# Products of constants in the first wait of the mixing stage and behind the sums of the output norms

## The chip, the cores and the metric

The kernel runs on one core of one Trainium2 chip. The time is that of one execution on the device, in microseconds; all rows below are of one profiled execution of the kernel before.

The core has a matrix engine (TensorE, PE in the profile; the loading of its weights is shown apart as PEld), a vector engine (DVE), a scalar engine (ACT), GpSimd (POOL), and SyncE (SP), which here only issues DMAs. The engines run side by side and wait for each other through semaphores. PE writes its results to PSUM, from which DVE and ACT read them. PE has a clock of two levels, 1.2 and 2.4 GHz; the profile shows which of them it was granted as 0.50 and 1.00.

## The reference

The kernel computes a hybrid decoder trunk of two layers on 256 tokens of width 1024, with 16 learned tokens ahead of them (T = 272). Each layer is a half-step SwiGLU feed-forward block, a token-mixing block, and a second half-step feed-forward block:

```
swiglu(x) = (silu(x @ w_gate) * (x @ w_up)) @ w_down
rms_norm(x, g) = x * rsqrt(mean(x * x) + EPS) * g
u = rms_norm(h, g_mix) @ w_in            # one projection, split into the inputs of four groups
A: rglru_mixer   B: gdn_mixer   C: ssd_mixer   D: s5_mixer
h = h + concat(yA, yB, yC, yD) @ w_out
```

The groups are a gated linear recurrence (A), a gated delta rule in chunks (B), a state-space scan in chunks (C) and a diagonal complex state-space model (D). Each ends in a norm of its own output: A over all its 512 channels, B over each of four heads of 128, C over two halves of 256. These are the output norms. All arithmetic is of float32 precision.

## The kernel before, in words

Activations lie with the channels on the 128 partitions and the tokens in the free dimension, so a product has 272 columns (256 in the second layer's end, where the learned tokens have been dropped). Weights stream in as pieces of 128x1024: SP loads `raw`, ACT rounds it to `hi` (L215), DVE takes the rest as `lo` (L217). A float32 product is made of three products of a reduced format that accumulate in one PSUM tile: `hi` with `xh` (L232), `hi` with `xl` (L233), `lo` with `xh` (L234); the helper is `mm3`. PSUM has eight banks: four for tiles `g` (weight products) and four for tiles `m` (all else, `s.mps()`).

The mixing stage is a list of steps, written out by hand. It begins with `first_tiles`, which puts the products of four output tiles on PE as far as the input is there, and then `norm_x` scales and splits the input: DVE multiplies (L315), ACT rounds (L316), DVE takes the rest (L317). The first four tiles are those of group D; DVE evicts them into `du` (L1158), which is stored and loaded again in another arrangement as `dU` (DMAs L1166 and L1168) and read by the products at L1179. The small tile of three scalar inputs per head is at L1290.

An output norm sums the squares over channels with products of one column (`token_sums`, L240: up to 128 tokens become the rows of the result, the constant `ones` is the moving operand). DVE adds epsilon (L251 or L253, tile `tok`), POOL takes the power of minus one half (L254, `toks`), PE brings the factor back to all partitions (`rstd_bc`, L262), and DVE multiplies (group A: L930; B: L777; C: L841). `ysplit` then rounds on ACT (L562, `s5a`) and takes the rest on DVE (L563, `s5b`), and the products of the output projection (`out_tiles`, L232 to L234) read these. In the list, the sums of a norm and its factor are separate steps (`an0` and `an1` for group A, `bo` with j = 0, 1, 2 for the heads of B, `cn` for C), with other work between them. Between the sums and the output products stand B's head products (L764 to L766), C's products (L826) and products of its decay (L517 to L525).

The order of the instructions on each engine comes from the list and from the framework's scheduler, which simulates the engines and moves instructions by priority. `issue_after(x)` pins what it encloses behind instruction x. The helper `fill` puts n products of the constant `onesr` (all ones) on PE, into a PSUM tile that nothing reads afterwards as such, behind `s.last_pe`. Before the change only `b_tail` set `s.last_pe`, and only `b_tail` with j = 1 called `fill`, with 5 products of 512 columns (L738).

PE runs its instructions in the order in which they are queued. The framework has a reader of a PSUM tile wait for the last PE instruction that wrote to the tile.

Of the kernel before, what the change touches and what calls it, by code (L numbers as in the profile page):

```python
# [16 lines left out]
P = 128  # L17
# [3 lines left out]
EPS = 1e-6  # L21
# [96 lines left out]
class Trunk:  # L118
# [110 lines left out]
    def mm3(s, ps, w, i, xh, xl, start, stop):  # L229
        nc = s.nc  # L230
        hi, lo = (t[:, i * P:(i + 1) * P] for t in w)
        nc.tensor.matmul(ps, lhsT=hi, rhs=xh, start=start, stop=False)  # L232
        nc.tensor.matmul(ps, lhsT=hi, rhs=xl, start=False, stop=False)  # L233
        nc.tensor.matmul(ps, lhsT=lo, rhs=xh, start=False, stop=stop)  # L234


    def token_sums(s, ps, acc, n, c=0, st=1):
        for b, o in enumerate(range(0, n, P)):
            w = min(P, n - o)
            s.nc.tensor.matmul(ps[0:w, c + b * st:c + b * st + 1], lhsT=acc[:, o:o + w], rhs=s.ones[:, 0:1], start=True, stop=True)  # L240


    def rstd_tok(s, ps, n, dim, eps, c=0, st=1):
# [18 lines left out]
            s.nc.tensor.matmul(pb[:, o:o + w], lhsT=rs[0:w, b:b + 1].to_broadcast([w, P]), rhs=s.ident[0:w, 0:w], start=True, stop=True)  # L262
        return pb[:, 0:n]

    def norm_tok(s, acc, n, dim, eps):
        ps = s.mps()
        s.token_sums(ps, acc, n)
        return s.rstd_tok(ps, n, dim, eps)

    def sumsq(s, acc, y, first, eng=None):  # L270
# [464 lines left out]
    def fill(s, ps, n):  # L735
        with s.tc.issue_after(s.last_pe):
            for _ in range(n):
                s.nc.tensor.matmul(ps, lhsT=s.onesr, rhs=s.onesr[:, 0:1].to_broadcast([P, 512]), start=True, stop=True)  # L738


    def b_tail(s, j):
# [16 lines left out]
    def b_out(s, h, l, j):  # L758
        nc = s.nc
        y = s.zb[:, h, :]  # L760
        if j == 0:
            ps = s.mps()
            n, o = s.N, T - s.N
            nc.tensor.matmul(ps[:, 0:n], lhsT=s.vs[:, 0, h, :], rhs=s.at[:, h, o:272], start=True, stop=False)  # L764
            nc.tensor.matmul(ps[:, 128 - o:n], lhsT=s.vs[:, 1, h, :], rhs=s.at[:, h, 272:416], start=False, stop=False)
            nc.tensor.matmul(ps[:, 256 - o:n], lhsT=s.vs[0:16, 2, h, :], rhs=s.at[0:16, h, 416:432], start=False, stop=True)  # L766
            t = s.buf('bt', [P, 4, T])[:, h, 0:n]
            nc.scalar.activation(out=t, in_=ps[:, 0:n], func=AF.Square)
            nc.vector.scalar_tensor_tensor(out=y, in0=ps[:, 0:n], scalar=s.gnh[:, l:l + 1], in1=y, op0=ALU.mult, op1=ALU.mult)
        elif j == 1:  # L770
            pn = s.mps()
            s.token_sums(pn, s.buf('bt', [P, 4, T])[:, h, :], s.N)
            s.bo[h] = s.rstd_tok(pn, s.N, 128, s.epq[:, :, h])
        else:
            pb = s.rstd_bc(s.bo[h], s.N)
            o = s.tmp()[:, 0:s.N]
            nc.vector.tensor_tensor(out=o, in0=y, in1=pb, op=ALU.mult)  # L777
            s.ysplit(o, 4 + h)
# [54 lines left out]

    def c_norm(s, g, l, j):
        if j == 0:
            s.cacc[g] = s.norm_tok(s.cacc[g], s.N, 256, 16 * EPS)
        else:
            pb = s.rstd_bc(s.cacc[g], s.N)
            for k in (2 * g, 2 * g + 1):
                o = s.tmp()[:, 0:s.N]  # L840
                s.nc.vector.scalar_tensor_tensor(out=o, in0=s.cy[:, k, :], scalar=s.col('snorm', l)[:, k:k + 1], in1=pb, op0=ALU.mult, op1=ALU.mult)  # L841
                s.ysplit(o, 8 + k)
# [78 lines left out]

    def a_norm(s, l, j):
        if j == 0:
            s.aacc = s.norm_tok(s.aacc, s.N, 512, 4 * EPS)
        else:
            s.ya = [s.rot([P, w], n, 1, F32R)[:, 0:4 * T] for n, w in (('s5a', 1840), ('s5b', 1792))]
            pb = s.rstd_bc(s.aacc, s.N)
            for i in range(4):
                o = s.tmp()[:, 0:s.N]
                s.nc.vector.scalar_tensor_tensor(out=o, in0=s.ag[:, i, :], scalar=s.col('lnorm', l)[:, i:i + 1], in1=pb, op0=ALU.mult, op1=ALU.mult)  # L930
                s.ysplit(o, i)
# [381 lines left out]
    def mixing(s, l, sl, done):  # L1313
        s.R, s.be, s.ce, s.bm, s.bo, s.cacc = ({} for _ in range(6))
        s5 = {}
        s.sl, s.N = sl, sl.stop - sl.start

        def small():
            s.sm16 = s.tokens(s.small_tile())

        def d_in(u):
            s5[u] = s.d_load(l, u)
            s.d_in(u, s5[u])

        def rin(i):
            s.R[i] = s.decay_in(i)

        def chain():
            with s.tc.issue_after(s.last_dve):
                s.b_chain()  # L1330

        do = dict(
            sm=small, tk=lambda: s.token_scalars(s.sm16, l), R=rin, S=lambda i: rin(2 + i),
            di=d_in, do=lambda u: s.d_out(u, s5[u]), da=lambda f: s.d_act(f, l), ds=s.d_split, dg=s.d_glu, dn=lambda j: s.d_norm(l, j),
            ks=lambda i: s.b_sums('k', i), qs=lambda i: s.b_sums('q', i), bn=lambda: s.b_norms(), bv=s.b_values, be=s.b_decay, bg=s.b_gram,
            bb=lambda: s.b_blocks(), bc=chain, bm=s.b_masks, bf=s.b_factor, bs=s.b_solve, bt=s.b_tail, bo=lambda h, j: s.b_out(h, l, j),
            xd=s.c_xdt, cg=s.c_gram, ce=s.c_decay, cp=lambda i: s.c_pair(i, l), cn=lambda g, j: s.c_norm(g, l, j),
            am=lambda i: s.a_gates(i, l), ac=lambda: s.a_coef(), an=lambda j: s.a_norm(l, j))
        do['as'] = s.a_scan
        full = slice(0, T)  # L1340
        pss = s.first_tiles(full)
        s.norm_x(s.col('nm', l), full)
        s.ahead(AHEAD)
        n, outs = 0, [0, 0]
        for name, a in STEPS:
            if name in IN:
                s.unit(name, a[0], pss[n] if n < NF else s.one_tile(sl if name in ('ag', 'bz', 'cz') else full), l)
                n += 1
            elif name in OUT:
                q = a[0]  # L1350
                s.out_tiles(q, OUT[name], outs[q] == 0, outs[q] == 3, sl, done)
                outs[q] += 1
            else:
                do[name](*a)
# [160 lines left out]
```

## Time and profile before

| | |
|---|---|
| median of 3 runs | 1443.67 us (1443.39 to 1445.18) |
| profiled execution | 1442.42 us |
| its span, from the first to the last instruction | 1440.5 us |
| mean granted clock of PE | 0.969 |
| PE busy | 1392.0 us, 97% of the span |
| DVE, ACT, POOL busy | 1036.4, 708.4, 205.4 us |
| L232, L233, L234 with `xh`, `xl` (2048 each) | 597.7, 595.3, 595.8 us |

The profile gives busy times by engine and line; a row of the timeline gives an instruction's start, its duration and, in brackets, how long its engine had been idle before it and for which instruction it had waited. PE instructions overlap: the time between the starts of two is what a product costs, and a duration holds its drain as well. A row with x4 is a run of four like instructions, its duration that of the run. The mixing stage of the first layer runs from about 235 to 500 us, that of the second from about 956 to 1215 us; the rest is feed-forward blocks.

### The profile page before, as it was taken

The page shows a single profiled execution, that of the slowest core. Times are in us where ns is not written, and L with a number is a line of the kernel's source. Part 1 is how long each engine was busy: PE and PEld are TensorE (multiplying, and loading weights), DVE is VectorE, ACT ScalarE, POOL GpSimd, SP SyncE. Part 2 cuts the span into 40 slices and gives each one's busy share as a digit, 9 for nine tenths or more (in the row PEclk, how much of TensorE's full clock was granted, in tenths as well). Part 3 has the DMA queues.
Part 4 walks back from the last instruction along what each step waited for, and adds up shares of the span by engine and source line. Part 5 has one row for each costly group of instructions (what it writes and reads, how often), then busy time and mean ns, then how long its engine had stood idle before and what let it go on. Part 6 is the DMA issues. An engine that isn't in the chain of part 4 may idle for free. (4 is left out here: it accounts for less than half of the span.)

```text
span 1440.5 us, 27604 instructions
## 1 busy us (share of the span) xinstructions
PE 1392.0 (97%) x10848; PEld 1353.8 (94%) x10848; DVE 1036.4 (72%) x1936; ACT 708.4 (49%) x1226; POOL 205.4 (14%) x235
## 2 busy tenths in 40 slices
PE   7999999998999999999999999999989899999997
PEld 7999998997998999999999999989989889999997
DVE  6998787978985468887656665669888746666653
ACT  6445444454675355554444444444555745544442
POOL 1000010322322320000100000103332223100011
PEclk9999999999997999999999999999999979999998
DMA  7568775654422256777555555556544213666662
GB/s 238 179 188 265 235 254 163 217 171 120 126 77 71 82 155 217 254 230 254 172 162 184 175 170 174 172 161 211 177 127 141 74 45 114 186 187 187 188 182 85
DMA packets 94025, 243.73 MB, mean 169 GB/s; under 512 B 29496, under 2 KB 39496, under 8 KB 93896
## 3 DMA queue, kind: packets, MB, share of 16 engines
q1 hardware_dynamic: 93896, 241.97, 54.2%
q8 instruction: 85, 1.39, 0.4%
q14 instruction: 44, 0.36, 0.1%
HBM read 222.16 MB, written 19.78 MB: 168 GB/s over the span
## 5 line engine op out<-in xcount | busy, mean ns | idle before, releaser
L215 ACT ACTIVATE hi<-raw 128x1024 fp32r<-128x1024 f32 (+1 forms) x382 | 403.3, 1056 | 532.2 <-PE g L233 302.0
L217 DVE TENSOR_TENSOR lo<-raw,hi 128x1024 fp32r<-128x1024 f32 (+1 forms) x382 | 470.2, 1231 | 215.6 <-ACT hi L215 213.9
L232 PE MATMUL g<-xh,hi 128*128 128x272 f32 (+1 forms) x2048 | 597.7, 293 | 12.2 <-ACT hi L215 8.7
L234 PE MATMUL g<-xh,lo 128*128 128x272 f32 (+1 forms) x2048 | 595.8, 292 | 0.8 <-DVE lo L217 0.8
L233 PE MATMUL g<-xl,hi 128*128 128x272 f32 (+1 forms) x2048 | 595.3, 291 | 0.3 <-DVE xl L317 0.3
L232 PEld LDWEIGHTS g<-xh,hi 128*128 128x128 f32 x2048 | 391.4, 191 | 14.7 <-ACT hi L215 8.6
L234 PEld LDWEIGHTS g<-xh,lo 128*128 128x128 f32 x2048 | 390.7, 191 | 2.6 <-DVE lo L217 1.1
L233 PEld LDWEIGHTS g<-xl,hi 128*128 128x128 f32 x2048 | 391.5, 191 | 1.5 <-DVE xl L317 0.6
L277 POOL TENSOR_TENSOR acc<-acc,r 128x272 f32<-128x272 f32 (+1 forms) x42 | 43.3, 1032 | 556.1 <-ACT r L276 555.4
L233 PE MATMUL g<-r,hi 128*128 128x272 f32 (+1 forms) x256 | 73.2, 286 | 0.0
L360 DVE TENSOR_TENSOR r<-r,g 128x272 f32<-128x272 f32 (+1 forms) x88 | 38.1, 432 | 37.5 <-PE g L234 36.0
L545 DVE SCALAR_TENSOR_TENSOR r<-g,small,r 128x269 f32<-128x269 f32 (+2 forms) x120 | 59.1, 493 | 2.0 <-ACT r L542 0.4
L234 PE MATMUL g<-ra,lo 128*128 128x272 f32 (+1 forms) x192 | 55.2, 287 | 0.0
L232 PE MATMUL g<-ra,hi 128*128 128x272 f32 (+1 forms) x192 | 55.1, 287 | 0.0
L233 PE MATMUL g<-rs,hi 128*128 128x272 f32 (+1 forms) x192 | 55.0, 286 | 0.0
L233 PE MATMUL g<-rz,hi 128*128 128x272 f32 (+1 forms) x192 | 55.0, 286 | 0.0
L234 PE MATMUL g<-rq,lo 128*128 128x272 f32 (+1 forms) x192 | 54.6, 287 | 0.0
L232 PE MATMUL g<-rq,hi 128*128 128x272 f32 (+1 forms) x192 | 53.5, 289 | 0.2
L358 DVE TENSOR_TENSOR r<-g,rstd 128x272 f32<-128x272 f32 (+1 forms) x88 | 38.3, 435 | 15.6 <-PE g L234 14.8
L233 PEld LDWEIGHTS g<-r,hi 128*128 128x128 f32 x256 | 48.1, 188 | 0.0
L232 PE MATMUL g<-dU,hi 128*128 128x272 f32 (+1 forms) x96 | 29.7, 309 | 9.8 <-DVE r L545 9.8
L359 ACT ACTIVATE r<-r 128x272 f32<-128x272 f32 (+1 forms) x88 | 36.5, 415 | 5.4 <-DVE r L358 4.2
(412 smaller groups left out, 2461.5 us busy)
## 6 DMA issues: line engine op xcount, KB each, us to landing
raw<-in_wgu_dram SPq DMA_DIRECT2D x176, 512.0 KB
raw<-in_wdn_dram SPq DMA_DIRECT2D x88, 512.0 KB
raw<-in_win_dram SPq DMA_DIRECT2D x80, 512.0 KB
raw<-in_wout_dram SPq DMA_DIRECT2D x32, 512.0 KB
s5a<-spill SPq DMA_DIRECT2D x8, 920.0 KB
s5b<-spill SPq DMA_DIRECT2D x8, 896.0 KB
spill<-s5a SPq DMA_DIRECT2D x8, 648.0 KB
spill<-rx SPq DMA_DIRECT2D x4, 640.0 KB
```

Source lines behind the costliest of these rows:

```text
L215: nc.scalar.activation(out=hi[:, 0:w], in_=raw[:, 0:w], func=AF.Copy)
L217: ins = nc.vector.tensor_tensor(out=lo[:, 0:w], in0=raw[:, 0:w], in1=hi[:, 0:w].bitcast(F32), op=ALU.subtract)
L232: nc.tensor.matmul(ps, lhsT=hi, rhs=xh, start=start, stop=False)
L233: nc.tensor.matmul(ps, lhsT=hi, rhs=xl, start=False, stop=False)
L234: nc.tensor.matmul(ps, lhsT=lo, rhs=xh, start=False, stop=stop)
L277: (eng or nc.gpsimd).tensor_tensor(out=acc, in0=acc, in1=t, op=ALU.add)
L358: nc.vector.tensor_tensor(out=t, in0=g[:, t0], in1=r, op=ALU.mult)
L359: nc.scalar.activation(out=si, in_=t, func=AF.Silu)
L360: nc.vector.tensor_tensor(out=a, in0=si, in1=u[:, t0], op=ALU.mult)
L545: nc.vector.scalar_tensor_tensor(out=dst[:, o:T], in0=ps[:, 0:T - o], scalar=taps[:, j:j + 1], in1=dst[:, o:T], op0=ALU.mult, op1=ALU.add)
```

## The change

`mm3` and `token_sums` now set `s.last_pe` too, and `fill` makes its products as wide as the PSUM piece it is given. Four products of 512 columns go into a fresh `m` tile between `first_tiles` and `norm_x`, in each layer. Three products of 384 columns go behind the sums of each output norm of groups A, B and C, into columns 128 to 511 of the sums' own PSUM tile: one group of three for A, four for B and two for C, so 7 groups in a layer. That makes 50 more products.

```diff
--- before.py
+++ after.py
@@ -231,13 +231,13 @@
         nc.tensor.matmul(ps, lhsT=hi, rhs=xl, start=False, stop=False)
-        nc.tensor.matmul(ps, lhsT=lo, rhs=xh, start=False, stop=stop)
+        s.last_pe = nc.tensor.matmul(ps, lhsT=lo, rhs=xh, start=False, stop=stop).ins
...
-            s.nc.tensor.matmul(ps[0:w, c + b * st:c + b * st + 1], lhsT=acc[:, o:o + w], rhs=s.ones[:, 0:1], start=True, stop=True)
+            s.last_pe = s.nc.tensor.matmul(ps[0:w, c + b * st:c + b * st + 1], lhsT=acc[:, o:o + w], rhs=s.ones[:, 0:1], start=True, stop=True).ins
@@ -262,9 +262,10 @@
-    def norm_tok(s, acc, n, dim, eps):
+    def norm_tok(s, acc, n, dim, eps, fill=0):
         ps = s.mps()
         s.token_sums(ps, acc, n)
+        s.fill(ps[:, 128:512], fill)
         return s.rstd_tok(ps, n, dim, eps)
@@ -735,7 +736,7 @@
     def fill(s, ps, n):
         with s.tc.issue_after(s.last_pe):
             for _ in range(n):
-                s.nc.tensor.matmul(ps, lhsT=s.onesr, rhs=s.onesr[:, 0:1].to_broadcast([P, 512]), start=True, stop=True)
+                s.nc.tensor.matmul(ps, lhsT=s.onesr, rhs=s.onesr[:, 0:1].to_broadcast([P, ps.shape[-1]]), start=True, stop=True)
@@ -770,6 +771,7 @@
             s.token_sums(pn, s.buf('bt', [P, 4, T])[:, h, :], s.N)
+            s.fill(pn[:, 128:512], 3)
...
-            s.cacc[g] = s.norm_tok(s.cacc[g], s.N, 256, 16 * EPS)
+            s.cacc[g] = s.norm_tok(s.cacc[g], s.N, 256, 16 * EPS, 3)
-            s.aacc = s.norm_tok(s.aacc, s.N, 512, 4 * EPS)
+            s.aacc = s.norm_tok(s.aacc, s.N, 512, 4 * EPS, 3)
@@ -1339,6 +1341,7 @@
         pss = s.first_tiles(full)
+        s.fill(s.mps(), 4)
         s.norm_x(s.col('nm', l), full)
```

Line numbers grow by one behind L265 and by two behind L773: the fill is at L738 before and at L739 after, the small tile at L1290 and L1292. Numbers in names count tiles and differ between the two kernels.

On PE, at the first wait of the first layer's mixing stage, the queue before reads as follows (`g_2960` is the last of the four first tiles, the other `g` tiles are the next ones):

```order
L234 MATMUL g_2960<-xh,lo_2954 128x272
L232 MATMUL g_2960<-xh,hi_2953 128x272
L233 MATMUL g_2960<-xl,hi_2953 128x272
L234 MATMUL g_2960<-xh,lo_2954 128x272
L232 MATMUL g_3134<-xh,hi_3106 128x272
L232 MATMUL g_3213<-xh,hi_3112 128x272
L1290 MATMUL g_3252<-xh,hi_3118 16x272
L233 MATMUL g_3134<-xl,hi_3106 128x272
```

Nothing stands between the last product of the first tiles and the first ones of the next. After the change, on the same engine at the same place:

```order
L234 MATMUL g_2960<-xh,lo_2954 128x272
L739 MATMUL m_3072<-onesr 128x512 x4
L232 MATMUL g_3139<-xh,hi_3111 128x272
L232 MATMUL g_3218<-xh,hi_3117 128x272
L1292 MATMUL g_3257<-xh,hi_3123 16x272
L233 MATMUL g_3139<-xl,hi_3111 128x272
```

The four products stand in the wait, and the rest is as it was. The second layer has them at the same place.

On PE, at the end of group B's solve and the sums of group A's norm (first layer), before (`m_5354` and `m_5447` are `b_tail`'s two tiles, `m_5516` that of the sums):

```order
L749 MATMUL m_5354<-rz_3283,rn_4060 16x128
L750 MATMUL m_5354<-rz_3283,rn_4060 16x128
L738 MATMUL m_5447<-onesr 128x512 x5
L764 MATMUL m_5498<-ra_4059,rs_4259 128x272
L765 MATMUL m_5498<-ra_4059,rs_4259 128x144
L826 MATMUL m_5504<-E_5042,rx_395 64x272 x2
L826 MATMUL m_5504<-E_5042,rx_395 64x144 x2
L826 MATMUL m_5504<-E_5042,rx_395 64x16 x2
L755 MATMUL m_5447<-rs_4259,a_72 16x128 x4
L240 MATMUL m_5516<-ones,cacc_5309 128x1 x2
L240 MATMUL m_5516<-ones,cacc_5309 16x1
L517 MATMUL m_5526<-r_5010,ugt 128x256
```

The five products stand behind the last of the pairs L749 and L750. After the change, from the first of these pairs on to the sums:

```order
L750 MATMUL m_5359<-rz_3288,rn_4065 16x128
L739 MATMUL m_5452<-onesr 128x512 x5
L751 MATMUL m_5359<-rz_3288,rn_4065 16x128
...
L756 MATMUL m_5452<-rs_4264,a_72 16x128 x4
L240 MATMUL m_5521<-ones,cacc_5314 128x1 x2
L240 MATMUL m_5521<-ones,cacc_5314 16x1
L739 MATMUL m_5521<-onesr 128x384 x3
L518 MATMUL m_5534<-r_5015,ugt 128x256
```

The old five products have moved seven products ahead, and three new ones stand behind the sums. Six more groups of this kind follow behind the other sums, and in the order after, the products of B's heads and C's (L765 to L767, L828) stand one by one between the first products of the output projection, where before they stood in one block behind 19 of them.

On PE, where the second layer's mixing stage reads `dU`, before (`g_11506` is a weight tile):

```order
L1290 MATMUL g_11472<-xl,hi_11338 16x272
L1290 MATMUL g_11472<-xh,lo_11339 16x272
L232 MATMUL g_11506<-xh,hi_11381 128x272
L233 MATMUL g_11506<-xl,hi_11381 128x272
L234 MATMUL g_11506<-xh,lo_11382 128x272
L232 MATMUL g_11506<-xh,hi_11381 128x272
L233 MATMUL g_11506<-xl,hi_11381 128x272
L234 MATMUL g_11506<-xh,lo_11382 128x272
L1179 MATMUL m_11399<-dU_7205,s5a_11395 128x68 x4
```

Six products of the tile stand ahead of L1179. After the change, at the same place:

```order
L233 MATMUL g_11537<-xl,hi_11412 128x272
L234 MATMUL g_11537<-xh,lo_11413 128x272
L232 MATMUL g_11537<-xh,hi_11412 128x272
L233 MATMUL g_11537<-xl,hi_11412 128x272
L234 MATMUL g_11537<-xh,lo_11413 128x272
L232 MATMUL g_11537<-xh,hi_11412 128x272
L233 MATMUL g_11537<-xl,hi_11412 128x272
L1181 MATMUL m_11430<-dU_7231,s5a_11426 128x68 x4
```

Thirteen products of that tile stand ahead of it there, of which the last seven are shown; in the first layer the order at this place is the same before and after.

## Rows read from the trace of the kernel before

**Rows 1.** Windows: stretch, length, busy time by engine, granted clock, DMA share, GB/s.

```profile
238.00:239.00 1.00, 0.76 (x3) 0.29 (x3) 1.00 (x4) 0.12 (x1) 0.00 (x0) 0.51 0.07 4
449.65:470.05 20.40, 20.07 (x74) 17.10 (x74) 5.06 (x17) 10.69 (x32) 6.97 (x9) 0.50 0.00 1
474.00:480.30 6.30, 6.30 (x55) 5.50 (x53) 4.58 (x12) 2.20 (x5) 5.39 (x6) 1.00 0.43 122
500.00:945.00 445.00, 445.00 (x3566) 441.85 (x3565) 301.05 (x439) 209.75 (x306) 22.30 (x29) 1.00 0.62 193
1166.45:1186.90 20.45, 19.04 (x69) 16.34 (x69) 4.75 (x15) 11.03 (x33) 5.71 (x5) 0.50 0.00 0
```

**Rows 2.** Timeline of PE: start, duration, engine, line, tiles, forms, idle before.

```profile
237.40 0.36 PE L232 MATMUL g<-xh,hi 128*128 128x272 f32 x1 [1.58 <-DVE du L1158]
...
238.95 0.59 PE L233 MATMUL g<-xl,hi 128*128 128x272 f32 x1
...
241.39 0.32 PE L234 MATMUL g<-xh,lo 128*128 128x272 f32 x1
...
249.46 0.78 PE L1179 MATMUL m<-dU,s5a 128*128 128x68 f32 x6
...
956.76 0.36 PE L232 MATMUL g<-xh,hi 128*128 128x272 f32 x1 [1.54 <-DVE du L1158]
...
969.89 1.97 PE L1179 MATMUL m<-dU,s5a 128*128 128x68 f32 x16 [0.39 <-DMA dU<-ud]
```

**Rows 3.** Timeline of PE at the first layer's output norms.

```profile
443.97 1.36 PE L738 MATMUL m<-onesr 128*128 128x512 f32 x5
...
448.01 0.74 PE L240 MATMUL m<-ones,cacc 128*128 128x1 f32 x6
...
449.43 0.44 PE L519 MATMUL m<-r,ugt 128*128 128x288 f32 x1
...
452.16 1.27 PE L764 MATMUL m<-ra,rs 128*128 128x272 f32 x2
...
454.38 1.27 PE L764 MATMUL m<-ra,rs 128*128 128x272 f32 x2
...
456.60 1.76 PE L262 MATMUL m<-cst,toks 128*128 128x128 f32 x6
...
459.41 1.27 PE L232 MATMUL g<-s5a,hi 128*128 128x272 f32 x4 [0.33 <-ACT s5a L562]
...
463.21 2.23 PE L240 MATMUL m<-ones,rz 128*128 128x1 f32 x12
465.37 0.59 PE L233 MATMUL g<-s5b,hi 128*128 128x272 f32 x1
...
469.84 0.77 PE L764 MATMUL m<-ra,rs 128*128 128x272 f32 x2
...
471.10 1.14 PE L826 MATMUL m<-E,rx 128*64 128x272 f32 x12
...
475.42 1.30 PE L240 MATMUL m<-ones,rz 128*128 128x1 f32 x12
...
477.72 1.03 PE L262 MATMUL m<-cst,toks 128*128 128x128 f32 x6
...
480.65 0.29 PE L519 MATMUL m<-r,ugt 128*128 128x288 f32 x1
...
482.27 0.77 PE L232 MATMUL g<-rq,hi 128*128 128x272 f32 x4
```

**Rows 4.** Chain that ended last, 955 to 975: start, duration, what.

```profile
964.89 4.87 DMA dU<-ud
```

**Rows 5.** Timeline of DVE at the first layer's output norms.

```profile
448.79 0.21 DVE L251 TENSOR_SCALAR tok<-m 128x2 f32<-128x2 f32 x2
...
458.39 1.72 DVE L930 SCALAR_TENSOR_TENSOR r<-dp,small,m 128x272 f32<-128x272 f32 x4 [7.92 <-PE m L262]
```

**Rows 6.** Timeline of PE at the second layer's output norms.

```profile
1176.74 0.58 PE L519 MATMUL m<-r,ugt 128*128 128x288 f32 x1 [1.42 <-DVE E L816]
```

## The prediction

> **What bounds the kernel now.** I read the windows first. In the stretch from 500 to 945, feed-forward blocks, PE is busy 445.00 of 445.00 us at a granted clock of 1.00, and 3566 products pass in it, 0.125 us each [rows 1]. There PE is the bound, so a product that is added to the path costs its full time, and what PE gains or loses in the mixing stage ahead of it comes out at the end. The windows then show where PE runs at the lower of its two clock levels (0.50, 1.2 GHz): about 1 us after the first wait of the mixing stage, where 238 to 239 has 0.51, and two long stretches at the output norms, 449.65 to 470.05 and 1166.45 to 1186.90, in which PE is busy 20.07 and 19.04 us, nearly always, and yet at 0.50 throughout [rows 1]. So the change meets three kinds of places: a wait in which PE does nothing, norm stages where it is busy at the lower level, and the same kind of work where it had the higher one.
>
> The timeline of PE says what went before each fall. In the first wait it had stood idle for 1.58 us (1.54 in the second layer) for DVE's eviction of `du` [rows 2]. At the norms it had not been idle. It ran six sums of one column from 448.01 on (0.74 us) and then B's decay from 449.43, and from 449.65 the clock is at 0.50 [rows 1, 3]. Yet from 474.00 to 480.30, with twelve such sums at 475.42 and six products L262 at 477.72, it is 1.00 all the time [rows 1, 3]; there weight products had filled PE behind C's products of 471.10. So such sums don't lower the clock wherever they stand: what lies around them decides, and products of constants are more of it.
>
> **The change part by part.** *First waits.* Four products of 512 columns cost 0.94 us (0.125 us for 272 columns gives 0.176 for 384 and 0.235 for 512). They fit into the idle 1.58 and 1.54 us, so they delay nothing: the products behind them wait for DVE, not for PE. If the clock stays, the 11 products from 238.95 to 241.39 take 1.38 instead of 2.44 us, 1.06 less [rows 2]. I take it that it stays: the pause shrinks to some 0.6 us. What is late next is `dU`. In the first layer L1179 starts at 249.46 without a wait of its own; in the second it waits 0.39 us for its reload, whose leg takes 4.87 us [rows 2, 4]. PE's clock doesn't bring the reload forward, since `du` hangs on DVE. In the first layer most of the gain becomes a wait there: I take -0.2 (bounds 0 and -1.06). In the second the order puts thirteen products instead of six ahead of L1179, 7 x 0.125 = 0.88 us, so PE comes there no sooner than now and keeps its gain: -1.0 (bounds 0 and -1.06). Sum -1.2.
>
> *A group of three at the norms* is 3 x 0.176 = 0.53 us at the higher level, 1.06 at the lower. In the first layer one group stands at 448.7, ahead of the fall, two behind the twelve sums at 463.21, four more behind 475; nothing covers them, since PE is busy there and stays the bound up to the end of the layer.
>
> *What the clock would give back*, if it stayed at 1.00 from 449.65 on, comes from like work at either level [rows 3]. B's decay products take 2.73 us from 449.43 to 452.16 and 1.62 from 480.65 to 482.27: 1.11 less, of which I take 0.9, since a first piece ran before the fall. The two blocks of B's head products take 2.22 each (452.16 to 454.38) against 1.26 (469.84 to 471.10): 1.92. Six products L262 take 1.76 against 1.03: 0.73. Four products L232 and B's decay again take 3.80 (459.41 to 463.21) against 4 x 0.125 + 1.62 = 2.12: 1.68. Twelve sums take 2.23 against 1.30: 0.93. Nineteen weight products take 4.47 (465.37 to 469.84) against 19 x 0.125 = 2.38: 2.09. Together 8.25 us. The second layer's stretch has the same length and pattern with 256 columns; I take the same sum.
>
> *Case by case, per layer.* Held throughout: 7 groups x 0.53 = 3.7 against 8.25, net -4.5. Held at first and lost in the wait behind L262: saved are 0.9 + 1.92 + 0.73 = 3.55; paid are 0.53 + 2 x 1.06 + 4 x 0.53 = 4.77; net +1.2. Lost as before: nothing saved, and 4.8 paid, net +4.8.
>
> *The wait behind L262* has no product of constants. The first L930 starts 1.8 us after L262 began, and PE's next product, L232, stands 0.33 us idle for ACT's rounding L562 [rows 3, 5]. At the higher level L262 and the two products behind it are over sooner, while DVE and ACT are not faster: from 458.39 to 459.41 their two steps take 1.02 us, of which PE would stand idle about 0.6 to 1.0. That lies between the idle 1.54 to 1.58 that lost the clock and the 0.39 at L1179 [rows 2]. In the second layer the products behind L262 stand idle 1.42 us for `E` [rows 6]. I count this as the point that decides, near to evens in each layer.
>
> *The norm's own chain.* DVE's `tok` (448.79, 0.1 us behind the sums) will wait for the last of the three products, as they go into the same tile: 0.53 us. Its factor L262 starts at 456.60, behind the two blocks of B [rows 3, 5]: DVE's 0.21 and POOL's power behind it leave some us in hand, and a faster PE, which comes to L262 about 2.3 us sooner, still leaves most of it. DVE then stands idle 7.92 us for L262 [rows 5], so nothing queued behind `tok` is pressed. I take 0 (at most 0.53 for the group). For B's sums the factor follows behind the weight products, at 477.72, 12 us later: 0.
>
> The row shows DVE reading the sums right behind PE. The Trainium skill ("PSUM — Partial Sum Buffer", section "PSUM bank collisions raise a hardware error") wants engines kept apart by bank and quadrant, not by address, which speaks against putting the products into columns 128 to 511 of the sums' tile: another address doesn't free DVE. By it, up to 7 x 0.53 = 3.7 us per layer could be added to the norm chains; by the rows it is hidden, for the first chain by the two blocks. No run here yet shows which.
>
> *Moved products.* `b_tail`'s five products move seven small products ahead; what `b_tail` does next doesn't come later by it: 0. B's head products and C's come earlier between the weight products of the output projection, also in PE's busy time: 0, with a bound of 1 us either way, as have the second layer's small changes of order on DVE, ACT and SP.
>
> **The sum.** One layer holds the clock and the other loses it behind L262: -1.2 - 4.5 + 1.2 = -4.5 us. The profiled execution took 1442.42 us (span 1440.5), so 1437.9; that execution lies 1.25 below the median of the runs, 1443.67, which gives 1439.2.
>
> **The rivals**, against the median:
> - *Both layers hold*: -1.2 - 9.0 = -10.2, 1433.5. For it: 474 to 480.3 has the same work and no product of constants, and held. Against it: the pauses behind L262 are unfilled.
> - *Both lose it behind L262*: -1.2 + 2.4 = +1.2, 1444.9. For it: the 1.42 us idle in the second layer, and the first four products there.
> - *One holds, one falls where it did*: -1.2 - 4.5 + 4.8 = -0.9, 1442.8. Three products are little against a stretch of several us of thin ones.
> - *The products only queue on a bound PE* (slower): the clock falls at the sums in both layers, or in one, with the other losing it later. Each layer then pays 4.8 (or 1.2 in that other): +8.4, 1452.1, or +4.8, 1448.5. For it: PE was busy at 0.50 for 20 us, so busy time alone doesn't keep the clock. It decides as soon as a norm stage is at 0.50 with its second and third group inside.
> - *The first waits don't keep the clock*: 1.2 worse in each case above; the pause that is left and the three partly idle products behind it speak for it. It shifts a case and makes none.
>
> **How the numbers follow.** Chances: forecast 0.36, both hold 0.25, both lose behind L262 0.12, one holds and one as before 0.10, the slower rival 0.17. The time is the forecast's, 1439.2; its own range, by the unknown moves and the first waits, is 1436 to 1443. The range for 8 in 10 reaches down through most of both-hold, 1431.5, and up into the slower rival, between its two sums, 1450. About 0.2%, 2.9 us, is what a measurement can tell here from no change: faster means below 1440.8, slower above 1446.6. Faster gets both-hold and some six tenths of the forecast, 0.45; the same gets the rest of the forecast and the two cases near zero, 0.29; slower gets the slower rival and the upper tail of those two, 0.26.
>
> **What would show it.** The clock in the windows 238 to 241 and 958 to 961 should be 1.00, and L1179 in the first layer should wait some 0.8 us for `dU`. At the norms the clock tells the case: 1.00 through both stretches, or a fall behind L262, or a fall at the sums. Products L240 and weight products next to each other should take their times at the level shown, and the three products 0.53 or 1.06. DVE's `tok` should begin some 0.5 us behind the sums and L262 wait for nothing. The forecast is wrong if the clock falls at the sums again, if the first waits still lose it, or if L262 comes to wait for `toks`.

## The result, and the profile after

The change makes the kernel slower: 1454.21 us median of 18 runs (1443.48 to 1459.21) against 1443.82 us of 18 runs before (1437.78 to 1450.27), ratio 1.0054, 95% interval 1.0037 to 1.0070. The ratio is not the quotient of the medians, which is 1.0072; executions of either kernel scatter by several us. Forecast were 1439.2 us and a range up to 1450. The profiled execution took 1457.68 us, with a span of 1456.0.

Windows of the changed kernel, columns as in [rows 1]:

```profile
238.00:241.00 3.00, 2.62 (x19) 2.11 (x19) 3.00 (x7) 0.00 (x0) 0.00 (x0) 1.00 0.60 172
250.90:257.70 6.80, 6.80 (x33) 6.80 (x32) 2.09 (x5) 0.35 (x2) 1.69 (x2) 0.50 0.34 134
455.70:476.20 20.50, 20.18 (x69) 16.55 (x67) 5.14 (x17) 10.97 (x33) 7.08 (x9) 0.50 0.00 1
1015.50:1025.70 10.20, 9.04 (x43) 9.04 (x43) 7.12 (x19) 4.86 (x14) 3.53 (x5) 0.50 0.71 234
1193.00:1199.80 6.80, 6.80 (x29) 6.62 (x29) 0.41 (x3) 1.72 (x7) 3.32 (x3) 0.50 0.00 0
```

Against [rows 1]: the first wait now runs at 1.00, and the 6.8 us from 250.9 on at 0.50, where the kernel before had 1.00. The first layer's norm stage has its 20.5 us at 0.50 as before. The second layer's has 6.8 instead of 20.45. The second layer's scan of group D has 10.2 us at 0.50, where the kernel before had 6.8:

```profile
1002.60:1009.40 6.80, 6.80 (x34) 6.80 (x33) 4.89 (x16) 4.85 (x14) 1.84 (x3) 0.50 0.85 278
```

PE's timeline at the first wait and at the reading of `dU`, columns as in [rows 2]:

```profile
235.54 1.03 PE L739 MATMUL m<-onesr 128*128 128x512 f32 x4
237.28 0.36 PE L232 MATMUL g<-xh,hi 128*128 128x272 f32 x1 [0.71 <-DVE du L1160]
...
250.26 3.09 PE L1181 MATMUL m<-dU,s5a 128*128 128x68 f32 x16 [1.88 <-DMA dU<-ud]
253.11 0.57 PE L234 MATMUL g<-xh,lo 128*128 128x272 f32 x1
```

The four products stand in the wait, as forecast, and the wait behind them shrinks from 1.58 to 0.71 us. PE is at the reading of `dU` by 248.38 and waits there 1.88 us, longer than the 1.06 us that the clock was to give, and behind that wait the clock falls: the sixteen products take 3.09 us and the next starts 2.85 us after the first.

PE's timeline at the first layer's output norms, then DVE's row that answers to the first of [rows 5], then the second layer's wait that answers to [rows 6]:

```profile
454.14 0.76 PE L739 MATMUL m<-onesr 128*128 128x384 f32 x3
454.74 0.39 PE L518 MATMUL m<-r,ugt 128*128 128x256 f32 x2
...
462.49 1.76 PE L262 MATMUL m<-cst,toks 128*128 128x128 f32 x6
...
470.33 1.32 PE L739 MATMUL m<-onesr 128*128 128x384 f32 x3
471.45 0.99 PE L240 MATMUL m<-ones,rz 128*128 128x1 f32 x6
...
483.27 0.76 PE L739 MATMUL m<-onesr 128*128 128x384 f32 x3
483.87 0.63 PE L240 MATMUL m<-ones,rz 128*128 128x1 f32 x6
```

```profile
454.94 0.21 DVE L251 TENSOR_SCALAR tok<-m 128x2 f32<-128x2 f32 x2 [0.68 <-PE m L739]
```

```profile
1190.26 0.37 PE L520 MATMUL m<-r,ugt 128*128 128x288 f32 x1 [1.60 <-DVE E L818]
```

A group of three costs PE 0.60 us at the higher level (454.14 to 454.74, 483.27 to 483.87) and 1.12 at the lower (470.33 to 471.45); forecast were 0.53 and 1.06. DVE waits 0.68 us for the group (forecast 0.53), and L262 stands without a wait, so that delay is hidden. The idle time that the forecast took as the point that decides is there (1.60 us in the second layer), and 2.7 us behind it the clock falls.

### The profile page after: what moved, and what is told of

Read it like the earlier page. It is cut to its first block, busy times and chain, and to the rows that moved or that the text cites. A ratio compares the mean times of both kernels' runs of the same rounds, so it can differ in the third digit from the quotient of the medians.

```text
span 1456.0 us, 27707 instructions
## 1 busy us (share of the span) xinstructions
PE 1402.8 (96%) x10898; PEld 1363.6 (94%) x10898; DVE 1037.0 (71%) x1936; ACT 708.0 (49%) x1226; POOL 204.6 (14%) x235
## 5 line engine op out<-in xcount | busy, mean ns | idle before, releaser
L361 DVE TENSOR_TENSOR r<-r,g 128x272 f32<-128x272 f32 (+1 forms) x88 | 38.0, 431 | 37.3 <-PE g L234 35.8
L359 DVE TENSOR_TENSOR r<-g,rstd 128x272 f32<-128x272 f32 (+1 forms) x88 | 38.1, 433 | 15.5 <-PE g L234 14.8
L552 ACT ACTIVATE r<-r 128x272 f32<-128x272 f32 x40 | 17.2, 429 | 47.4 <-DVE r L546 30.9
```

Of the source, the lines that this page charges most:

```text
L359: nc.vector.tensor_tensor(out=t, in0=g[:, t0], in1=r, op=ALU.mult)
L361: nc.vector.tensor_tensor(out=a, in0=si, in1=u[:, t0], op=ALU.mult)
L552: nc.scalar.activation(out=t, in_=x, func=AF.Tanh, scale=0.5)
```

## The experiments

Every kernel was run 6 to 18 times in turns with the kernel before. Beside time and ratio the table has two figures that each run gives: its time at 0.50, which is 2 x (1 - mean granted clock) x span, and the time without the clock's loss, which is the time less half of that (an estimate: it takes PE as the bound wherever the clock is low). Both are means over the runs. The kernel before was run anew beside each later batch: its medians there are 1443.98 to 1445.69, and 1398.7 to 1400.0 without the loss. A difference by the means is taken against the runs of before that stood beside the same kernel.

| kernel | median us | ratio, 95% interval | at 0.50 | without the loss |
|---|---|---|---|---|
| before (29 runs beside E1 to E4) | 1444.18 | 1 | 88.8 | 1399.8 |
| the change | 1454.21 | 1.0054 (1.0037 to 1.0070) | 82.3 | 1412.5 |
| E1 first waits only | 1445.88 | 1.0013 (0.9990 to 1.0037) | 90.8 | 1400.9 |
| E2 groups only | 1446.97 | 1.0027 (0.9998 to 1.0055) | 77.4 | 1409.2 |
| E3 moved five only | 1448.00 | 1.0023 (1.0000 to 1.0046) | 96.2 | 1399.8 |
| E4 the change again | 1455.96 | 1.0091 (1.0055 to 1.0128) | 86.3 | 1413.4 |
| E5 the change, five unmoved | 1446.11 | 1.0015 (0.9996 to 1.0035) | 73.3 | 1410.4 |
| E6 group A's sums only | 1442.31 | 0.9977 (0.9957 to 0.9998) | 79.7 | 1401.6 |
| E7 as E6, and four behind L262 | 1438.55 | 0.9953 (0.9932 to 0.9975) | 66.1 | 1404.7 |
| E8 groups of six only | 1456.24 | 1.0077 (1.0061 to 1.0094) | 74.6 | 1418.2 |
| E9 the change, no first waits | 1451.00 | 1.0051 (1.0028 to 1.0073) | 77.0 | 1411.9 |
| E10 E2, five moved in layer 2 | 1447.46 | 1.0030 (1.0001 to 1.0059) | 79.1 | 1408.4 |
| E11 five behind the sums | 1451.96 | 1.0059 (1.0035 to 1.0083) | 99.6 | 1401.6 |
| E12 as E7, with six | 1434.66 | 0.9946 (0.9919 to 0.9974) | 63.1 | 1404.2 |
| E13 the change, first wait in layer 1 only | 1452.25 | 1.0043 (1.0016 to 1.0071) | 78.1 | 1412.2 |
| E14 the same, in layer 2 only | 1453.75 | 1.0049 (1.0022 to 1.0075) | 79.8 | 1412.7 |
| E15 before again | 1444.74 | 0.9986 (0.9964 to 1.0008) | 87.7 | 1400.3 |
| E16 E12 again | 1436.34 | 0.9938 (0.9913 to 0.9962) | 64.3 | 1403.4 |
| E17 E2, five moved in layer 1 | 1449.72 | 1.0028 (1.0004 to 1.0052) | 77.7 | 1411.0 |
| E18 E5 again | 1450.36 | 1.0030 (1.0005 to 1.0054) | 80.6 | 1409.6 |

### E1 to E4: the parts alone

In E1, E2 and E5 the sums and the weight products set another attribute (`last_mm`), behind which the new products go, so `b_tail` keeps its place:

```diff
-        s.last_pe = nc.tensor.matmul(ps, lhsT=lo, rhs=xh, start=False, stop=stop).ins
+        s.last_mm = nc.tensor.matmul(ps, lhsT=lo, rhs=xh, start=False, stop=stop).ins
...
+        s.fill(s.mps(), 4, s.last_mm)      # E1, E5
+        s.fill(ps[:, 128:512], fill, s.last_mm)      # E2, E5
```

> Only the four products in each first wait; everything else as before the change. Theory 1 (early arrival at dU): the clock stays at 1.00 from 238 to 241, PE comes to L1179 about 1 us sooner, waits there 1 to 2 us for dU in the first layer, and the clock falls behind that wait; the time is 2 to 5 us longer than before. Theory 2 (the norms' products carry the whole loss): no fall at dU that costs more than it saves, time 0 to 2 us shorter. Theory 3 (the moved five products and the new order carry it): same as theory 2.

> Only the groups of three behind the sums; the five products of b_tail stay where they were before, and the first waits have none. Theory 1: the clock falls at the sums or behind L262 as it did before, 3 to 5 us more per layer where it falls at the sums and about -1 to +1 where it falls later; 4 to 8 us longer in all. Theory 2: 8 to 10 us longer. Theory 3: within 3 us of before.

E3 is the change without any new product; E4 the change itself.

> No new products; only the place of b_tail's five products and the order that the scheduler makes of it. Theories 1 and 2: within 2 us of before. Theory 3: 5 to 10 us longer, with the loss at the output norms and behind.

> The changed kernel once more, for a second profile of it. Theory 1: PE again waits over 1 us for dU in the first layer and the clock falls there; norms cost 3 to 5 us in a layer where the clock falls at the sums. If the places of the falls are chance, the wait at L1181 is there but the fall is not, and the layers differ from the first profile by several us each way; the time is 6 to 12 us above before in any case.

No part alone is clear of no change; E3's interval ends at it. E1 gains nothing: its time at 0.50 is about that of before. E2 has what the forecast was made for: the time at 0.50 falls by 11.4 us, which is worth 5.7, and 9.4 are paid for it. E3 pays nothing and has 7.4 us more at 0.50. Theories 2 and 3 fall as single causes: no part carries the loss, and the three means, 2.0, 3.6 and 3.6 us over before, come to about what the change costs, 9.2. E1's profile doesn't test theory 1: both first waits lost the clock in spite of the products (3.4 us each, from 239.3 and from 966.4), and PE didn't wait for `dU`. E4 has the wait for `dU` again, 1.99 us, with the fall behind it.

### E5, E18: the change without the moving

> The change, but with b_tail's five products where they stood before. Theory 1 (three separate costs that add: the first waits 2.0 us, the groups at the norms 3.6, the moved products 3.6): 5 to 6 us longer than before, and 3 to 5 us shorter than the changed kernel. Rival (the moved products cost nothing by themselves, the changed kernel's loss is that of the new products): as slow as the changed kernel, 9 to 10 us longer than before.

> The change with b_tail's five products where they stood before, a second sample and profile. Theory: the second layer's stretch from the small tile to the first b_tail product takes 200 to 203 us, PE waits for dz as in the kernel before; 2 to 4 us longer than before. Rival (the first sample was lucky): 5 us longer than before or more, that stretch over 204 us.

E5 and E18 are 2.7 and 4.4 us over before by their means (1447.0 and 1450.0 against 1444.3 and 1445.5), less than the 5 to 6 that E5's theory added up: new products alone cost some 3.6 us, and the moving in their company 4 to 7 more, up to the mean of the change (1453.7). E18's stretch in the second layer took 206.3 us, against the expectation, though PE's wait for `dz` is short; it waited 2.7 us for `dU` there, and the clock fell behind that wait too.

### E9, E10, E17: what the moving does

E9 is the change without the products in the first waits. E10 and E17 have the groups, and the move in one layer:

```diff
+        s.mv = l == 1      # E10; 0 in E17
+        if s.mv:
+            s.last_pe = s.last_mm
```

> The changed kernel without the products in the first waits: the groups of three and the moved five, in the changed kernel's order on every engine. Theory 1 (the first waits' products give little, 0 to 2 us either way; moving the five with the groups present costs the rest): 7 to 10 us longer than before, as the changed kernel within 2 us. Rival (the early arrival at dU makes the changed kernel slow): 3 to 5 us longer than before, like the groups alone.

> The groups of three, with b_tail's five products moved ahead in the second layer alone; the order on DVE, ACT, POOL and SP is that of the groups alone but for two rows. Theory 1a (the moving itself costs, by its place in each layer): 1.5 to 4 us longer than the groups alone, 5 to 8 longer than before. Theory 1b (what costs is the new order of the second layer's B and weight products, which comes with the moving in the first layer): within 1.5 us of the groups alone, 2.5 to 5 longer than before.

> The groups of three, with b_tail's five products moved ahead in the first layer alone. That move brings the changed kernel's new order of the second layer on all engines with it, the move in the second layer does not. Theory (the new order of the second layer is what costs, not the moving): the stretch from the second layer's small tile to its first b_tail product takes 204 to 206 us as in the five profiles with the new order, not 200 to 203 as in those without; PE waits over 3 us for dz there; 5 to 8 us longer than before, 2 to 4 longer than with the move in the second layer alone. Rival (the place of the five in the first layer costs at the norms): that stretch as before, the first layer's norm stage 3 us longer.

Moved in the second layer the five cost nothing over E2 (3.9 us over before against 3.6, by the means). Moved in the first layer, they make the scheduler order the second layer anew on PE, DVE and ACT, as it is in the change. The waits of PE from 960 to 1050, for `dz` of POOL (us in total, times, longest), in the change, in E17 and in E18, which has the old order there:

```profile
PE m L1217 <- POOL dz L1187: 4.5, 4, 1.7
```

```profile
PE m L1220 <- POOL dz L1190: 4.4, 4, 2.2
```

```profile
PE m L1217 <- POOL dz L1187: 2.2, 3, 0.9
```

In the six profiles with the new order this wait is 4.4 to 4.6 us, in the fourteen without 2.2 to 2.8 (2.5 in the kernel before), and the 2 us between are about what E9, E17 and the change (1411.0 to 1412.5) have over E2, E5 and E18 (1409.2 to 1410.4) without the clock's loss. Behind the longer wait the clock falls:

```profile
1003.05:1013.20 10.15, 9.04 (x42) 8.85 (x42) 7.70 (x19) 4.85 (x14) 4.12 (x5) 0.50 0.73 231
```

That is E17; all six profiles with the new order have 10.2 us at 0.50 at this place in one piece, no other has. The stretch from the second layer's small tile to its first `b_tail` product takes 204.3 to 208.6 us (mean 205.4) with it and 199.2 to 206.3 (mean 202.0) without. By time alone E17 doesn't show the cost: it is 4.4 us over before, short of the 5 to 8 expected, and E10 is 3.9 over. Taken together the times do show it: the six kernels with the new order (E4, E9, E13, E14, E17 and the change) are 4.4 to 12.3 us over before (mean 7.7), the four runs with groups of three and the old order (E2, E5, E10, E18) 2.7 to 4.4 (mean 3.7). How much of these 4 us is the order, and how much the place of the five in the first layer, is not parted.

### E13, E14: the first waits in one layer

```diff
+        if l == 0:      # E13; 1 in E14
+            s.fill(s.mps(), 4)
```

> The changed kernel with the four products in the first wait of the first layer alone; every other instruction in the same order. Theory 1 (in the first layer PE then comes early to dU, waits about 1.9 us there and the clock falls for two stretches behind it, where without them it falls once at the first wait): as slow as the changed kernel, 2 to 4 us longer than it is without any first-wait product. Rival (the difference between the changed kernel and the one without first-wait products is chance): within 1.5 us of the one without.

> The changed kernel with the four products in the first wait of the second layer alone. Theory 1 (there thirteen products stand ahead of the read of dU, PE hardly waits, and the gain of about 1 us stays): 0 to 2 us shorter than without any first-wait product, 3 to 5 us shorter than the changed kernel. Rival (chance): as the other one, within 1.5 us of the changed kernel without first-wait products.

Over before, E13 and E14 are 6.3 and 7.7 us by the means, E9 is 6.3: neither is clear of E9, and theory 1 falls for both. Whether the change's own 3 us over E9 (9.2) are more than chance stays open. What the profiles agree on is the place: in the first layer the clock held through the first wait in 8 of 20 profiles, and in these 8, and only there, PE then waited more than 1 us for `dU` (1.23 to 2.12). In 6 of the 8 the clock fell behind that wait for 6.8 us. The products in the first wait do what they should, the clock held in 5 of the 6 profiles that have them there and in 3 of the 14 others. But holding gives nothing back: from the first product behind the first wait to the last product L755 of `b_tail` the 8 profiles took 214.6 to 217.0 us (mean 215.7), the other 12 took 210.2 to 217.2 (mean 213.0). E6, without such products, held and lost the clock behind `dU` on its own:

```profile
249.86 3.50 PE L1180 MATMUL m<-dU,s5a 128*128 128x68 f32 x16 [1.81 <-DMA dU<-ud]
```

In the second layer the clock held through the first wait in 5 of the 6 profiles with products there and in 2 of the 14 others. With thirteen products ahead of the read (the change, E4, E14) PE then waited 0.1 to 0.83 us for `dU` and no fall followed, as the forecast argued. With six to eight ahead (E5, E8, E12, E18) it waited 1.78 to 2.71 us, and in three of these four the clock fell there.

### E15: the same instructions, another profile

> The kernel before, for a second profile of the same instructions. If the falls of the clock at the norms belong to the instructions, as the prediction took them, the second profile has 20 us at 0.50 at the norms of either layer again. If they shift from execution to execution, the norm stages have another count of low stretches, by several us of time each way, with no instruction changed. The time is that of before within 1 us.

Windows of E15 in the second layer's norm stage, and of E1, whose PE instructions there are those of the kernel before, in the same order (E3's too):

```profile
1165.50:1168.70 3.20, 3.20 (x20) 2.55 (x19) 1.43 (x4) 2.52 (x7) 0.71 (x1) 1.00 0.00 0
1168.75:1172.10 3.35, 3.35 (x10) 2.50 (x9) 0.00 (x0) 2.76 (x10) 1.18 (x1) 0.50 0.00 0
1172.20:1175.50 3.30, 1.70 (x12) 1.49 (x12) 2.24 (x7) 2.08 (x6) 0.66 (x1) 1.00 0.00 0
1175.55:1185.75 10.20, 10.20 (x43) 9.11 (x41) 1.98 (x8) 4.08 (x12) 3.33 (x3) 0.50 0.01 2
```

```profile
1173.80:1184.80 11.00, 9.39 (x58) 7.75 (x56) 5.46 (x16) 9.86 (x29) 2.65 (x2) 1.00 0.00 0
1184.85:1188.20 3.35, 3.35 (x17) 3.35 (x17) 0.34 (x2) 1.38 (x6) 3.25 (x3) 0.50 0.02 5
```

Where the profile of before had 20.45 us at 0.50, E15 has 13.7 and E1 3.4, with no instruction changed there. So the falls do not belong to the instructions alone. Read from the start of the last product L755 of `b_tail` to the start of the layer's last product L826 of C (line numbers of the kernel before), the norm stages took, with the time at 0.50 within:

| | first layer | second layer |
|---|---|---|
| before | 39.8 us, 20.5 | 35.9 us, 20.5 |
| E15 | 39.9, 20.5 | 33.9, 13.7 |
| E1, E3 (each) | 42.7, 27.3 | 29.3, 3.4 |
| mean of these four | 41.3, 23.9 | 32.1, 10.3 |
| the change | 43.3, 20.5 | 34.2, 6.8 |
| E4, E9 | 39.9 and 39.8, 10.2 | 34.2, 6.8 |
| mean of the ten with groups of three | 41.6, 15.7 | 34.0, 6.5 |
| the least at 0.50 in any of the ten | 6.8 | 3.4 |
| E8 | 38.1, 0.0 | 38.0, 6.8 |
| E6, E7 | 43.3, 27.3 and 41.1, 20.5 | 31.4, 6.8 and 28.7, 0.0 |
| E12, E16 | 37.3, 10.2 and 34.4, 3.4 | 29.2, 0.0 (each) |

### E6 to E8, E12, E16: how many products, and where

```diff
+        s.fill(ps[:, 128:512], fill, s.last_mm)      # a_norm alone: 3 in E6 and E7, 6 in E12 and E16
             pb = s.rstd_bc(s.aacc, s.N)
+            s.fill(s.mps(), 4, s.last_mm)      # E7, E12, E16: behind L262 of group A's norm
```

> Only the group of three behind the sums of group A's norm, one in each layer; no other group, none in the first waits, nothing moved. Theory 1 (a group costs its 0.53 us at the bound PE, and it is this first group that keeps the clock up): the time apart from the low clock grows by about 1 us instead of 9, the time at 0.50 falls by most of the 11 us that all groups gave; 2 to 5 us shorter than before. Rival (the later groups keep the clock, or the gain is chance): the time at 0.50 as before, the whole 0 to 2 us longer.

> As the kernel with the group behind group A's sums alone, and four products of 512 columns more behind the products L262 of that norm, in the wait that no product fills in the changed kernel. Theory 1 (the clock is lost in that wait): no fall behind L262, time at 0.50 some 15 to 25 us less than before, 5 to 8 us shorter in all. Rival (the four products only delay L232 and B's decay, and the clock falls elsewhere in the stretch): within 2 us of the kernel with the one group, or up to 2 us longer.

> The groups at the norms alone, of six products instead of three, nothing moved. Theory 1 (each product costs its width at the bound PE): the time apart from the low clock grows by 42 x 0.176 = 7.4 us over that of the groups of three, the time at 0.50 falls by 5 to 10 us; 3 to 5 us longer than the groups of three. Rival (the cost is mostly the longer wait of DVE for the sums' tile, which is the same chain whatever its length): 1 to 2 us longer than the groups of three.

> Six products behind the sums of group A's norm instead of three, and the four in the wait behind L262. Theory 1 (with more products the first fall at the sums, which three still let through in one layer of the profile, goes too): time at 0.50 another 5 to 15 us less than with three, 8 to 11 us shorter than before. Rival (three are enough where the clock can be kept at all, and three more only queue, 2 x 0.53 us): 5 to 6 us shorter than before.

> The version with six products behind group A's sums and four behind its L262 once more, for a second sample: 7 to 10 us shorter than before if the first was no chance; 2 to 6 if it was a lucky draw.

E8 doubles the price: 9.0 us more than E2 without the clock's loss for 42 more products, 0.21 each, against 0.20 in the rows (0.60 for three). Its time at 0.50 hardly falls further (74.6 against 77.4), so it is 7.6 us slower than E2 by the means, more than either expectation. E6 keeps a good part of the clock for 6 products instead of 42, by the mean of its runs (79.7 at 0.50); its one profile, with 27.3 and 6.8 us at the norms, doesn't show where. E7 and E12 add the four in the wait behind L262, and are the fastest: E12 and E16, two samples, by 0.54% and 0.62%. Six instead of three at the sums is not clear of chance (E12 against E7), and the four in the wait without products at the sums weren't run. Timeline and windows of E12:

```profile
448.56 1.25 PE L739 MATMUL m<-onesr 128*128 128x384 f32 x6
...
454.46 1.03 PE L262 MATMUL m<-cst,toks 128*128 128x128 f32 x6
455.42 1.14 PE L739 MATMUL m<-onesr 128*128 128x512 f32 x4
456.61 0.50 PE L518 MATMUL m<-r,ugt 128*128 128x256 f32 x2
```

```profile
447.70:472.20 24.50, 24.44 (x173) 20.82 (x170) 11.40 (x33) 14.28 (x38) 11.88 (x13) 1.00 0.07 22
472.35:482.50 10.15, 10.15 (x40) 8.99 (x39) 2.31 (x8) 2.40 (x7) 3.83 (x4) 0.50 0.14 52
1161.80:1191.00 29.20, 28.23 (x210) 24.29 (x207) 15.18 (x40) 17.91 (x48) 12.18 (x10) 1.00 0.12 37
```

L262 starts 5.9 us behind the first product of constants (8.35 in the change, 454.14 to 462.49), and the wait behind it is filled. The second layer's stage has no fall, in E7, E12 and E16 alike. PE's wait for `E` there is 0.96 to 0.97 us in these three, where it is 1.60 in the change; the row is E12's:

```profile
1170.83 0.48 PE L518 MATMUL m<-r,ugt 128*128 128x256 f32 x2 [0.97 <-DVE E L817]
```

### E11: the old five behind the sums

```diff
-            s.fill(ps, 5)      # b_tail
+        s.fill(ps[:, 128:512], 5, s.last_mm)      # a_norm, j == 0
```

> No product more than before: b_tail's five products of 512 columns are left out, and five of 384 stand behind the sums of group A's norm instead. Theory 1 (the place of the five decides how often the clock falls at the sums: ahead of them it costs, behind them it gives): the time at 0.50 falls by 8 to 15 us, 3 to 6 us shorter than before. Rival (five at either place keep the clock equally, the gain of the one group came from having more products): within 1.5 us of before.

Theory 1 falls, and the rival with it: 0.59% slower than before, with the most time at 0.50 of all. PE's wait that the five had filled, and the stage behind it:

```profile
451.89 1.50 PE L755 MATMUL m<-rs,a 16*16 16x128 f32 x8 [1.63 <-DVE rs L752]
```

```profile
452.40:482.90 30.50, 30.18 (x113) 24.28 (x112) 7.14 (x23) 12.12 (x36) 8.37 (x10) 0.50 0.00 1
```

The old five stood in a wait of their own, and behind the sums they don't replace it. They were no spare products.

## Why the prediction was wrong

In the table's terms the forecast paid 8.5 us (groups of three, partly at the lower level) and got 13.0 back (11.8 at the norms, 1.2 in the first waits). The change pays 12.7 (1412.5 against 1399.8) and gets 3.2 back, half of 88.8 less 82.3. With the 0.41 us for each us at 0.50 that the runs of before show (last section), it pays 12.1 and gets 2.7.

By place, in the two profiles of each kernel (us; the norm stages as in the table under E15, the stretches ahead of them from the first product behind the first wait):

| | before, E15 | the change, E4 | difference of the means |
|---|---|---|---|
| first layer, ahead of the norms | 210.4, 211.5 | 216.0, 217.0 | 5.6 |
| first layer, norm stage | 39.8, 39.9 | 43.3, 39.9 | 1.8 |
| second layer, ahead of the norms | 208.3, 207.1 | 215.5, 211.3 | 5.7 |
| second layer, norm stage | 35.9, 33.9 | 34.2, 34.2 | -0.7 |
| all else | 946.1, 945.9 | 947.0, 947.6 | 1.3 |

So most of the loss lies ahead of the norms, where the forecast had a gain of 1.2. Two profiles are few, as the clock's falls move several us. Over all twenty, the first layer's stretch ahead of the norms is 2.4 us longer with products in its first wait (six profiles against fourteen), the second's 3.6 longer with the new order (six against fourteen), and the norm stages 0.3 and 1.9 longer with groups of three: 8.2 of the 9.2 us. By place the forecast had -0.2, -1.0 and -3.3. All three steps failed.

**The clock given back at the norms: -3.3 forecast, +2.2 found.** The forecast took the 20.4 us at 0.50 in each layer of the one profile as the kernel's, priced their removal at 8.25 us per layer and let the change collect 11.8. The second layer's 20.5 were a bad draw: the same instructions have 3.4 to 20.5 there, 10.3 on average over four profiles. Compared with that average, the ten profiles with groups of three have 0.3 and 1.9 us longer stages, with 8 and 4 us less at 0.50. Two of the three cases came as described: the fall at the sums (the change, and six of the ten in the first layer) and the fall behind L262 (four of the ten there, and all ten in the second layer). The third, held throughout, which the forecast counted on for one layer, came in none of these twenty stages. So the wait behind L262, rightly named as the point that decides, was not near to evens: left unfilled behind groups of three, it lost the clock wherever the sums had not, and with the four products in it (E7, E12, E16) the second layer held. Only E8's first layer, with six behind every sum, held with the wait unfilled. The prices were nearer. Against the profile of before, held-and-lost was -1.7 in the second layer (forecast +1.2; the fall lasted 6.8 us there and not to the stretch's end), and the fall at the sums +3.5 in the first (forecast +4.8, of which 0.5 lie behind this stretch).

**The groups' price** was near: 0.60 for 0.53, 8.4 us for 14 groups, more where the clock is low; E2 paid 9.4.

**The first waits: -1.2 forecast, nothing found.** In the change's profile the clock held as forecast, and `dU` was named as late next. But the wait there was costed at the gain alone. In the first layer the clock also falls behind it, where it had held before. Against the kernels without them, E1, E13 and E14 are 0 to 2 us slower, none clear of zero.

**The moved products and the new order: 0 with 1 us either way was too small.** The order of the second layer was seen before the run (thirteen products ahead of L1181 instead of six) and counted as cover for the first wait's gain. It lengthens the wait for `dz` by 2 us in all six profiles that have it, with a longer fall behind it. E3, which is not clear of no change, has no new order and could lose by the clock alone; why the place of the five would cost there isn't shown, since E3's profile and E1's have the same falls at the norms.

**The norm's chain** stayed hidden, as forecast: L262 waits for nothing. DVE did wait 0.68 us for a group that it doesn't read, so other columns of the tile didn't free it; the framework sets that wait by the tile. It didn't come out in the time of this chain. The Trainium skill ("PSUM — Partial Sum Buffer", section "PSUM bank collisions raise a hardware error") wants PSUM guarded by bank and quadrant, not by address; no run here tests that, as the two never met. A kernel with the products in a tile of their own wasn't run.

**The rival on the other side** (products queue on a bound PE) had the right mechanism, one of several, and 0.17 as its chance; faster had 0.45. Its smaller sum, 1448.5, is the case that the change's profile shows at the norms; that the time came out 6 us above even this is the work of the stretches ahead. Where one profile is the only base and the effect hangs on a clock that falls at other places in each execution, that was too sure.

Open stays how much each part costs to better than 1.5 us: the means of twelve runs have errors of 1.0 to 1.6 us, and the parts don't add exactly (2.7 and 4.4 for first waits and groups together, against 2.0 + 3.6).

## What to carry to other kernels

Products that are to hold the clock paid here once in front of the fall and in the wait behind which it fell (six and four per layer: 0.5 to 0.6%); put behind every sum on a bound engine they were a tax (42 products cost 9.4 us and gave 5.7). Before pricing what a clock's fall costs, profile the same kernel a second time: what a second profile moves can't be counted as a gain. And after filling a wait, look at the next one on the same engine, and at what the scheduler did to a stage far behind.

## What the runs showed that was not expected

The clock's falls shift between executions of the same instructions: the second layer's norm stage has 20.5 and 13.7 us at 0.50 in two profiles of one kernel, and 3.4 in E1 and E3, whose PE instructions there are the same. The lost time and the time at 0.50 go together over the runs: over 29 runs of the kernel before, the time rises by 0.41 us for each us at 0.50 (0.37 to 0.39 in the other batches), somewhat less than the half that a PE-bound stretch would give.
